# Keys and queries of a gated delta rule turned by VectorE instead of TensorE, gates as one ScalarE operation, and a new order of the mixer's work

## The chip, the cores and the metric

The kernel runs on one core of one Trainium2 chip. The metric is the device time of one execution in microseconds (us), the median of several runs. The engines are TensorE (PE; its weight loads are listed as PEld), VectorE (DVE), ScalarE (ACT), GpSimd (POOL) and SyncE (SP), which only issues transfers here.

## What is computed

One decoder layer of 512 tokens and width 1024: a SwiGLU feed-forward block, a hybrid mixer and a second feed-forward block, each behind an RMS norm. Of the reference, the part of the mixer that the change touches:

```python
q_h = jax.nn.silu(hq) * HG_DK ** -0.5                       # HGRN branch, 8 heads
o_h = rmsnorm(o_h, hgrn_out_norm) * jax.nn.silu(hg)
qkv = jax.nn.silu(causal_short_conv(concat(gq, gk, gv), conv_w))   # 4 taps, 32 heads of 128
q_g = l2norm(cq) * GDN_DK ** -0.5                           # 8 query and 8 key heads
k_g = l2norm(ck)
o_g = gated_delta_chunked(q_g, k_g, cv, sigmoid(gb), g)     # 16 value heads, chunks of 64
o_g = rmsnorm(o_g, gdn_out_norm) * jax.nn.silu(gz)
y = sigmoid(gate_h) * (o_h @ w_branch_hgrn) + sigmoid(gate_g) * (o_g @ w_branch_gdn)
```

Here l2norm(x) = x * rsqrt(sum(x*x) + EPS) over the 128 elements of a head.

## The kernel before

**Stages.** The first feed-forward block runs from 0 to about 355 us, the mixer to about 1240 us, the second block to the end. Activations lie with features on partitions and 512 tokens in the free dimension. Dense products are made in three passes (fp32 split into a high and a low part): high by high (L192), low by high (L193) and high by low (L194), each a 128x128 weight tile against 512 tokens (256 in the feed-forward blocks and the HGRN values). A weight tile of 128x512 is loaded by SP into one of RB = 3 `raw` places, then split: ACT casts the high part (`whi`, L1868), DVE subtracts to give the low part (`wlo`, L1870); WB = 6 such pairs exist. A cast waits until PE has done with the pair that it overwrites. A dense product goes to one of two PSUM banks (tag "mm", tile `pmm`), which ACT or DVE must read before the next but one may start.

**Order in the mixer.** The whole mixer is written out in an order that the class `Desk` makes while the program is built. Each piece of work is a generator ("thread") that asks for events ("on"), for places ("get": the six 128x512 tiles "ta", PSUM banks, buffers), or for an engine for a booked time ("use", with `A`, `V` and `T_` giving ACT, DVE and PE); "lag" lets time pass, as for a transfer. `Desk.run` always takes the engine and thread that can start first by these booked times, and instructions stand on each engine in that order. Dense products have the lowest rank on PE and come in the order of the string `DENSE` (F, Q, D, B are HGRN projections; k, q, v, z those of the delta rule; y merge gates), as far as `choose` finds their needs met. PE work marked `Patient` lets dense work go first for up to WAIT = 4 us.

**The delta rule (GDN).** Eight pairs u = 0..7, each one key/query head and two value heads. `conv` (L1168) copies a projection out of PSUM (`ci`, L1174), does the first tap on ACT (`cy`, L1181), three more on DVE (L1184), a Tanh on ACT (L1187) and finishes SiLU on DVE as (tanh+1)*y (L1193, L1196); a value head is then turned by DVE (`turn`, L1205) and bounced through DRAM (`bounce`: SP stores it and loads it back turned, with LAG["turn"] = 6.5 us booked for each). `norms` turns each key and query head on PE (four 128x128 transposes into `ptk`, L1245); ACT copies the keys (`kn`, L1248) and squares four blocks with a row sum (L1252). `g_e` makes the decays: Abs and one Exp for each head. Then come the 64x64 inverses by doubling (`pq`, copies L1398 to L1419), and the recurrence over chunks (`pks`, `pw`, `pog`). At the end of a pair, ACT scales the output (L1535, four instructions for a head); for pairs 0 to 6 DVE turns it and it is bounced, for the last pair PE turns it (`pto`, L1549), DVE gates it (`on`, L1552), and ACT (`uh`, L1561) and DVE (`ul`, L1563) split it into slices 14 and 15 of the input of the closing product with `wbg`. Slices that were stored earlier come back as `og` and are split at L1653 and L1655. `zgate` (L1605) and `gate` (L1623) make SiLU of the output gates, again by Tanh on ACT and a second operation on DVE.

Of the kernel before, what the change touches and what calls it, by code (L numbers as in the profile page):

```python
# [11 lines left out]
AF = mybir.ActivationFunctionType  # L12
ALU = mybir.AluOpType
# [3 lines left out]
P = 128  # L17
# [14 lines left out]
LEVELS = (1, 2, 4, 8, 16)  # L32

DENSE = (
# [3 lines left out]
)  # L38
MERGE = (None, None, "a", "a", "b", "b", None, None)
WB = 6  # L40
# [13 lines left out]
FRESH = 5  # L54
LAG = dict(raw=3.5, gb=6.5, nb=6, m=7, out=6.5, back=6, turn=6.5)
EASE = 2.5
LANES = {"a": 2, "b": 2, "d": 1, "e": 1}


# [7 lines left out]
class Desk:  # L67
# [3 lines left out]


    def __init__(self, **places):
        self.left, self.at, self.idle, self.now = dict(places), {}, {}, 0.0
        self.busy, self.asked, self.cur, self.dense = [], [], None, False

    def start(self, rank, gen):
# [660 lines left out]
def mixer(tc, mp, e):  # L738
# [11 lines left out]
    def v3(ap, a):  # L750
        return ap.rearrange("p (a b) -> p a b", a=a)
# [165 lines left out]
    def h_q(i, pt, new):  # L917
        tag = ("fs", "ut")[i % 2]
        if new:
            yield "get", "ta", 1  # L920
            yield *A(512), 1
            th = ta("th")
            act.activation(th, pt, AF.Tanh, scale=0.5)
            yield "get", tag, 1
            yield *V(560), 1
            qq = hq[i] = place(tag, "qq", (P, NT, 192), 4)
            dve.scalar_tensor_tensor(qq[:, :, :P], v3(th, NT), 1.0, v3(pt, NT), op0=ALU.add, op1=ALU.mult)
            D.put("mm")
            D.put("ta")
            D.fire(("Q", i))  # L930
            return
        yield "get", "ta", 2
# [4 lines left out]
        D.put("mm")  # L937
        yield A(512)
        th = ta("th")
        act.activation(th, qs, AF.Tanh, scale=0.5)  # L940
        yield "get", tag, 1
        yield V(512)
        qq = hq[i] = place(tag, "qq", (P, NT, 192), 4)
        dve.scalar_tensor_tensor(qq[:, :, :P], v3(th, NT), 1.0, v3(qs, NT), op0=ALU.add, op1=ALU.mult)
        D.put("ta", 2)
        D.fire(("Q", i))

    def h_f(i, pt, new):
# [33 lines left out]
    def h_head(i):  # L982
# [151 lines left out]
        dve.tensor_scalar(rho, ss, 4.0 / P, 4.0 * EPS * 4.0 * P, op0=ALU.mult, op1=ALU.add)  # L1134
# [34 lines left out]
    def conv(k, i, pt, out, n):  # L1169

        yield "get", "ta", 2
        yield *A(512), 1
        ci = ta("ci", (P, T + 32))[:, :T + 3]
        act.copy(ci[:, 3:], pt)  # L1174
        D.put("mm")
        yield V(4)
        dve.memset(ci[:, :3], 0.0)
# [3 lines left out]
        act.activation(y, ci[:, :T], AF.Copy, scale=wc[0])  # L1181
        for j in range(1, 4):
            yield V(550)
            dve.scalar_tensor_tensor(y, ci[:, j:j + T], wc[j], y, op0=ALU.mult, op1=ALU.add)  # L1184
        yield A(512)
        th = ci[:, :T]
        act.activation(th, y, AF.Tanh, scale=0.5)  # L1187
        a, b = (v3(th, n), v3(y, n)) if n else (th, y)
        if k[0] in "qk" and k[1] > 3:
            yield "on", ("K", k[1] - 4)  # L1190
        yield V(512)
        if n:
            dve.scalar_tensor_tensor(out, a, 1.0, b, op0=ALU.add, op1=ALU.mult)  # L1193
            D.put("ta", 2)
        else:
            dve.scalar_tensor_tensor(y, a, 1.0, b, op0=ALU.add, op1=ALU.mult)  # L1196
            yield V(512)
            turn(th, y)
            D.put("ta")
            yield from bounce(f"vn{i}", th, out, "ta")  # L1200
        D.fire(k)

    def turn(out, x):

        dve.transpose(out.rearrange("p (f c j) -> p f c j", f=4, c=NT), x.rearrange("p (c i f) -> p f c i", c=NT, f=4))  # L1205
# [12 lines left out]

    def g_e(u, st):

        yield "on", "decays", *([("at", 2 * u + 1)] if u < 2 else ["more"]), *([("R", u - 4)] if u > 3 else []), \
            *([("E", u - 1)] if u else [])
        for i in range(2):
            hd_ = 2 * u + i
            yield "get", "gb", 1
            yield "use", "ACT", .1
            gb = places["gb"]("gb", (P, NT, P))
            act.dma_start(gb, gtd[hd_:hd_ + 1].rearrange("o (c b) -> o c b", c=NT).to_broadcast([P, NT, P]))
            yield "lag", LAG["gb"]
            a = G["at"][u % 4 * 2 + i]  # L1230
            for c in range(NT):
                yield A(200)
                act.activation(a[:, c], gb[:, c], AF.Abs, bias=gam[:, c, hd_:hd_ + 1], scale=-1.0)
            D.put("gb")
            yield A(512)
            act.activation(a, a, AF.Exp, scale=-1.0)
        D.fire(("E", u))

    def norms(u, i, kq, kn, sm):
        yield "on", ("kq"[i], u)  # L1240
        yield "get", "e", 1
        yield T_(Patient(.5))
        pt = ps("ptk", "e")
        for c in range(NT):
            pe.transpose(pt[:, c * P:(c + 1) * P], kq[:, c, i], ident)  # L1245
        if i == 0:
            yield A(512)
            act.copy(kn, v3(pt, NT))  # L1248
        for c in range(NT):
            yield A(300)  # L1250
            pc = pt[:, c * P:(c + 1) * P]
            act.activation(pc, pc, AF.Square, accum_out=sm[:, 0, 4 * i + c:4 * i + c + 1])  # L1252
        D.put("e")
        D.fire(("norm", u, i))

    def g_n(u, st):
# [9 lines left out]
        hs = slice(2 * u, 2 * u + 2)  # L1266
        rk = sm[:, 1, 0:4]
        yield V(4)
        dve.tensor_scalar(rk, sm[:, 0, 0:4], 4.0 * EPS, None, op0=ALU.add)
# [10 lines left out]
        dve.tensor_scalar(c2, c2, 0.5, None, op0=ALU.mult)  # L1280
        D.fire(("C", u))
        yield "on", ("q", u)
        yield "on", ("qm", 0), ("n2", u % 2)
# [145 lines left out]
    def g_rec(u, st):  # L1429
# [34 lines left out]
        for c in range(NT):  # L1464
# [36 lines left out]
            if c < NT - 1:  # L1501
# [5 lines left out]
                else:  # L1507
                    for i in range(2):
# [12 lines left out]
        dve.tensor_scalar(sm[:, 7, 0:4], sm[:, 0, 4:8], 4.0 * P * EPS, 16.0 * P * EPS * EPS, op0=ALU.mult, op1=ALU.add)  # L1521
        dve.scalar_tensor_tensor(v3(rho, 2), v3(ss, 2), 4.0 / P, sm[:, 7:8, 0:4].to_broadcast([P, 2, 4]),
                                 op0=ALU.mult, op1=ALU.add)
        yield "lag", EASE
        yield "use", "POOL", 1.4
# [79 lines left out]
    def zgate(i, pt):  # L1605

        g = G["gz"][i // 2 % 3].rearrange("p c b -> p (c b)")[:, i % 2 * T:i % 2 * T + T]
        yield *A(512), 1
        act.activation(g, pt, AF.Tanh, scale=0.5)
        yield *V(560), 1  # L1610
        dve.scalar_tensor_tensor(g, g, 1.0, pt, op0=ALU.add, op1=ALU.mult)
        D.put("mm")
        D.fire(("z", i))

# [7 lines left out]

    def gate(key, g, t, o):  # L1623

        yield "get", "thg", 1
        yield A(300)
        th = places["thg"]("thg", (P, 256))
        act.activation(th, o, AF.Tanh, scale=0.5)
        yield V(256)
        dve.scalar_tensor_tensor(g[:, t], th, 1.0, o, op0=ALU.add, op1=ALU.mult)  # L1630
        D.put("thg")
        D.put("mm")
        if t == 3:
            D.fire(key)
# [464 lines left out]
```

## Time and profile before

| | us |
|---|---|
| median of 3 runs | 1596.22 (1595.67 to 1598.09) |
| the profiled execution's own time | 1595.04 |
| its span | 1593.3 |
| PE busy | 1580.1 (99%) |
| DVE busy | 1140.4 (72%) |
| ACT busy | 843.1 (53%) |
| POOL busy | 407.7 (26%) |

The span reaches from the first to the last profiled instruction; the run's own time is 1.7 us longer. A row of a group view gives line, engine, operation, output<-input, count, then busy time in us, mean ns of one, and the idle time of the engine ahead of it with what ended it. Matmuls overlap: in a steady stream one of 128x512 starts every 0.23 us, though its row says 0.39. In rows of single instructions, the bracket holds the idle time ahead and its releaser.

### The profile page before, as it was taken

The page shows a single profiled execution, that of the slowest core. Times are in us where ns is not written, and L with a number is a line of the kernel's source. Part 1 is how long each engine was busy: PE and PEld are TensorE (multiplying, and loading weights), DVE is VectorE, ACT ScalarE, POOL GpSimd, SP SyncE. Part 2 cuts the span into 40 slices and gives each one's busy share as a digit, 9 for nine tenths or more (in the row PEclk, how much of TensorE's full clock was granted, in tenths as well). Part 3 has the DMA queues.
Part 4 walks back from the last instruction along what each step waited for, and adds up shares of the span by engine and source line. Part 5 has one row for each costly group of instructions (what it writes and reads, how often), then busy time and mean ns, then how long its engine had stood idle before and what let it go on. Part 6 is the DMA issues. An engine that isn't in the chain of part 4 may idle for free.

```text
span 1593.3 us, 28865 instructions
## 1 busy us (share of the span) xinstructions
PE 1580.1 (99%) x10464; PEld 1368.1 (86%) x10464; DVE 1140.4 (72%) x2217; ACT 843.1 (53%) x1905; POOL 407.7 (26%) x715
## 2 busy tenths in 40 slices
PE   9999999999999999999999999999999999999997
PEld 8899998888888888888878888888788899999886
DVE  6988786448858769746788988875545799888323
ACT  5756674335334344645776666665324566667322
POOL 0211212000312222065635776610001121121000
PEclk9999999999999999999999999999999999999999
DMA  5777873333213213555345536566544587787431
GB/s 183 168 163 158 177 172 97 118 114 113 81 54 94 57 51 101 153 156 152 109 140 166 151 120 191 180 202 215 153 141 132 135 199 183 173 183 194 135 102 53
DMA packets 144751, 223.90 MB, mean 141 GB/s; under 512 B 22224, under 2 KB 44368, under 8 KB 144608
## 3 DMA queue, kind: packets, MB, share of 16 engines
q1 hardware_dynamic: 127472, 191.15, 38.8%
q0 software_dynamic: 14400, 26.22, 10.5%
q10 hardware_dynamic: 2736, 4.68, 1.0%
q8 instruction: 82, 1.34, 0.3%
q14 instruction: 61, 0.50, 0.1%
HBM read 197.06 MB, written 24.94 MB: 139 GB/s over the span
## 4 chain that ended last, share of the span: by engine, by line
PE 88%; DVE 4%; DMA 3%; issue 2%; ACT 1%; POOL 0%; SPq 0%; POOLq 0%; DVEq 0%; ACTq 0%
PE pmm L192 16%; PE pmm L193 15%; PE pmm L194 15%; PE px L194 6%; PE px L192 6%; PE px L193 6%; PE pnat L192 4%; PE pnat L194 4%; PE pnat L193 4%; DMA wlo<-w1b 1%; PE pgq L1291 1%; PE pog L1499 1%; PE pw L1483 1%; PE pl L1054 1%; DMA raw<-wt 1%
## 5 line engine op out<-in xcount | busy, mean ns | idle before, releaser
L192 PE MATMUL pmm<-uh,whi 128*128 128x512 f32 x834 | 343.6, 412 | 1.4 <-ACT ci L1174 1.4
L194 PE MATMUL pmm<-uh,wlo 128*128 128x512 f32 x834 | 326.3, 391 | 0.0
L193 PE MATMUL pmm<-ul,whi 128*128 128x512 f32 x834 | 325.6, 390 | 0.5 <-DVE ul L1655 0.3
L194 PE MATMUL px<-xs,wlo 128*128 128x256 f32 x1008 | 285.9, 284 | 0.7 <-DVE wlo L311 0.3
L193 PE MATMUL px<-xs,whi 128*128 128x256 f32 x1008 | 285.2, 283 | 0.0
L192 PE MATMUL px<-xs,whi 128*128 128x256 f32 x1008 | 285.2, 283 | 0.0
L1868 ACT CAST whi<-raw 128x512 fp32r<-128x512 f32 x226 | 140.0, 620 | 219.1 <-PE pmm L193 184.1
L1870 DVE TENSOR_TENSOR wlo<-raw,whi 128x512 fp32r<-128x512 f32 x226 | 162.2, 719 | 115.4 <-ACT whi L1868 110.7
L194 PEld LDWEIGHTS px<-xs,wlo 128*128 128x128 f32 x1008 | 193.4, 192 | 1.6 <-DVE wlo L311 0.8
L192 PEld LDWEIGHTS px<-xs,whi 128*128 128x128 f32 x1008 | 193.5, 192 | 0.1
L193 PEld LDWEIGHTS px<-xs,whi 128*128 128x128 f32 x1008 | 193.5, 192 | 0.1
L194 PEld LDWEIGHTS pmm<-uh,wlo 128*128 128x128 f32 x834 | 156.5, 188 | 34.5
L192 PEld LDWEIGHTS pmm<-uh,whi 128*128 128x128 f32 x834 | 157.0, 188 | 32.5 <-ACT ci L1174 2.0
L193 PEld LDWEIGHTS pmm<-ul,whi 128*128 128x128 f32 x834 | 157.2, 188 | 29.8 <-DVE ul L1655 0.6
L332 ACT CAST whi<-sw 128x512 fp32r<-128x512 f32 x144 | 87.5, 613 | 91.6 <-DVE sw L369 72.3
L332 ACT CAST whi<-rw 128x512 fp32r<-128x512 f32 x153 | 94.3, 617 | 76.2 <-PE pnat L194 42.9
L311 DVE TENSOR_TENSOR wlo<-sw,whi 128x512 fp32r<-128x512 f32 x144 | 98.2, 682 | 0.0
L332 ACT CAST whi<-raw 128x512 fp32r<-128x512 f32 x71 | 42.5, 601 | 91.9 <-PE pmm L193 41.1
L337 POOL DMA_DIRECT2D wlo<-w1b x53 | 45.9, 867 | 168.7 <-ACT wlo L336 107.8
L311 DVE TENSOR_TENSOR wlo<-raw,whi 128x512 fp32r<-128x512 f32 x67 | 51.1, 778 | 48.4 <-ACT whi L332 48.4
L1342 POOL TENSOR_TENSOR fm<-gfs,gln 128x60 f32<-128x60 f32 (+24 forms) x155 | 65.8, 425 | 63.5 <-DMA gln<-hmask 42.1
L337 POOL DMA_DIRECT2D wlo<-w1a x47 | 40.9, 870 | 159.6 <-ACT wlo L336 128.5
(489 smaller groups left out, 3324.1 us busy)
## 6 DMA issues: line engine op xcount, KB each, us to landing
raw<-wt SPq DMA_DIRECT2D x160, 256.0 KB
rw<-w1b SPq DMA_DIRECT2D x80, 256.0 KB
rw<-w1a SPq DMA_DIRECT2D x74, 256.0 KB
wlo<-w1b POOLq DMA_DIRECT2D x53, 256.0 KB, 5.3
wlo<-w1a POOLq DMA_DIRECT2D x47, 256.0 KB, 5.0
raw<-w2a SPq DMA_DIRECT2D x36, 256.0 KB
raw<-wn SPq DMA_DIRECT2D x32, 256.0 KB
raw<-wbg SPq DMA_DIRECT2D x32, 256.0 KB
```

The source lines that it names most:

```text
L192: pe.matmul(pt, ah, bh, start=first, stop=False)
L193: pe.matmul(pt, ah, bl, start=False, stop=False)
L194: pe.matmul(pt, al, bh, start=False, stop=last)
L311: dve.tensor_tensor(lo, x, hi.bitcast(F32), op=ALU.subtract)
L332: act.copy(hi, x)
L337: pool.dma_start(lo, units[i].fold, accum_op=ALU.add)
L1054: pe.matmul(pl_[s0:s0 + 32, c * 16:(c + 1) * 16], ke[:, c * P + s0:c * P + s0 + 32], qv[:, c, r, :, 1], start=True, stop=True)
L1291: pe.matmul(pq[:, (c % 2) * 256:(c % 2) * 256 + 256], kq[:, c, 0], kq[:, c].rearrange("p a b -> p (a b)"), start=True, stop=True)
L1342: pool.tensor_tensor(tv, bc(m[:, j + 1:, j], w), t[:, j:j + 1, :w].to_broadcast([P, n, w]), op=ALU.mult)
L1483: pe.matmul(pw[:, hd2[i]], ut[:, 4 * i + c], xs[i], start=True, stop=True)
L1868: act.copy(hi, raw)
L1870: dve.tensor_tensor(lo, raw, hi.bitcast(F32), op=ALU.subtract)
```

## The change

1. **Order string.** `DENSE` is rewritten: in the HGRN part F and Q are no longer strictly in turn, and in the GDN part keys come ahead of queries.
2. **Desk.** A place used to be counted. Now `left` keeps the time at which each one comes free (the time of the thread that gave it up), and a thread that takes it cannot start before.
3. **SiLU in one operation.** `h_q`, `conv`, `zgate` and `gate` use ACT's Silu and no second DVE operation. Constants that had made up for the factor 2 of (tanh+1)*y change with it.
4. **First tap.** It moves from ACT (Copy with a scale) to DVE (tensor_scalar).
5. **Keys and queries.** With TURNED = (0, 1), `norms` no longer uses PE and PSUM: DVE turns the head into a "ta" tile `kt`, SP stores it and loads it back, ACT copies the keys from there and squares from there. The "ta" place is held from the turn to the last square.
6. **Decays.** The two Exp of a pair stand behind one booking of 4 us on ACT.

```diff
     def put(self, tag, n=1):
-        self.left[tag] += n
+        self.left[tag] += [self.cur.t if self.cur else self.now] * n
+        self.left[tag].sort()
...
-                elif kind == "get" and self.left[what[0]] >= what[1]:
-                    self.left[what[0]] -= what[1]
-                    th.t = max(th.t, self.now)
+                elif kind == "get" and len(self.left[what[0]]) >= what[1]:
+                    th.t = max([th.t, self.now] + self.left[what[0]][:what[1]])
+                    del self.left[what[0]][:what[1]]
...
-        yield A(512)
+        yield V(512)
         y = ta("cy")
-        act.activation(y, ci[:, :T], AF.Copy, scale=wc[0])
+        dve.tensor_scalar(y, ci[:, :T], wc[0], None, op0=ALU.mult)
...
-        yield A(512)
-        th = ci[:, :T]
-        act.activation(th, y, AF.Tanh, scale=0.5)
...
-        yield V(512)
+        yield A(512)
         if n:
-            dve.scalar_tensor_tensor(out, a, 1.0, b, op0=ALU.add, op1=ALU.mult)
+            act.activation(out, v3(y, n), AF.Silu)
...
-            yield A(512)
+        yield "use", "ACT", 4.0
+        for i in range(2):
+            a = G["at"][u % 4 * 2 + i]
             act.activation(a, a, AF.Exp, scale=-1.0)
...
+        if i in TURNED:
+            yield "get", "ta", 1
+            yield V(900)
+            x = ta("kt")
+            turn(x, kq[:, :, i])
+            yield from bounce(f"{'kq'[i]}n{u}", x, x)
+            x4 = x.rearrange("p (r c j) -> p c r j", r=4, c=NT)
+            if i == 0:
+                yield A(512)
+                act.copy(kn.rearrange("p c (r j) -> p c r j", r=4), x4)
+                D.fire(("kc", u))
+            for c in range(NT):
+                yield A(300)
+                act.activation(x4[:, c], x4[:, c], AF.Square, accum_out=sm[:, 0, 4 * i + c:4 * i + c + 1])
+            D.put("ta")
+            D.fire(("norm", u, i))
+            return
...
     def gate(key, g, t, o):
-        yield "get", "thg", 1
         yield A(300)
-        th = places["thg"]("thg", (P, 256))
-        act.activation(th, o, AF.Tanh, scale=0.5)
-        yield V(256)
-        dve.scalar_tensor_tensor(g[:, t], th, 1.0, o, op0=ALU.add, op1=ALU.mult)
-        D.put("thg")
+        act.activation(g[:, t], o, AF.Silu)
```

In whole numbers, from the two orders: PE's matmuls go from 9074 to 9010 (the 64 transposes into `ptk`), with the dense ones 7552 in both; the places at which small matmuls stand between dense ones go from 192 to 198; ACT's table loads go from 5 to 27; DVE's turns from 94 to 110; transfers issued by SP from 781 to 813. A line of code gets another number: L192, L193, L194 become L194, L195, L196; L1174 becomes L1168, L1187 becomes L1183, L1245 and the `ptk` operations have no successor on PE, L1535 becomes L1545, L1549 becomes L1559, L1561 becomes L1571, L1868 becomes L1871. Where the changed order says `x_...` or `h`, it is a shared buffer under the name of its first user.

On PE, before the change, the closing product with `wbg` at the mixer's end. `pto` is the turned head; the three products behind the shown group, on `uh` and `ul`, are the thirteenth slice, then come the fourteenth and fifteenth, made from the two turned heads. The other group of transposes stands 15 matmuls ahead of this one:

```order
L194 MATMUL pmm<-uh,wlo 128x512
L1549 MATMUL pto<-sq,on 128x128 x4
L192 MATMUL pmm<-uh,whi 128x512
L193 MATMUL pmm<-ul,whi 128x512
L194 MATMUL pmm<-uh,wlo 128x512
L192 MATMUL pmm<-uh,whi 128x512
```

The same place on PE with the change: the thirteenth slice, a group of transposes, the fourteenth slice, a group of transposes, the fifteenth:

```order
L194 MATMUL pmm<-uh,whi 128x512
L195 MATMUL pmm<-ul,whi 128x512
L196 MATMUL pmm<-uh,wlo 128x512
L1559 MATMUL pto<-sq,on 128x128 x4
L194 MATMUL pmm<-uh,whi 128x512
L195 MATMUL pmm<-ul,whi 128x512
L196 MATMUL pmm<-uh,wlo 128x512
L1559 MATMUL pto<-sq,on 128x128 x4
L194 MATMUL pmm<-uh,whi 128x512
```

Each turned head is now used by the very next dense matmul; before, the first was used 18 dense matmuls after it was turned and the second six.

On ACT, before the change, early in the GDN part, where the keys of a pair are copied (`x_8168<-ptk`), the 64x64 inverse of the pair ahead is copied (`acc`, `h`), an output is scaled (`gat`), and a projection leaves PSUM (`ci<-pmm`):

```order
L1248 COPY x_8168<-ptk 128x512
L1252 ACTIVATE ptk,sm<-ptk 128x128
L1868 CAST whi<-raw 128x512
L1410 COPY acc<-pq_9012 128x256
L1252 ACTIVATE ptk,sm<-ptk 128x128 x3
L1181 ACTIVATE cy<-ci,cs 128x512
L1419 COPY h<-pq_9052 64x4x64
L1868 CAST whi<-raw 128x512
L1174 COPY ci<-pmm 128x512
```

The same place on ACT with the change:

```order
L1871 CAST whi<-raw 128x512
L1244 COPY x_8031<-kt 128x512
L1545 ACTIVATE gat<-gat,sm 128x128 x4
L1420 COPY acc<-pq_8872 128x256
L1248 ACTIVATE kt,sm<-kt 128x4x32
L1871 CAST whi<-raw 128x512
L1545 ACTIVATE gat<-gat,sm 128x128 x4
L1429 COPY h<-pq_8916 64x4x64 x2
L1183 ACTIVATE h<-cy 128x4x128
L1168 COPY ci<-pmm 128x512
```

Two outputs of four scalings each now stand among these rows, between a cast and the copy that frees a PSUM bank. The cast at the top overwrites a pair whose last reader on PE stands about 18 dense matmuls ahead of the matmul that needs this bank. The copy of the keys and the squares read `kt`, which a transfer has to bring, where they read PSUM before.

More of the change, by code (lines that the diff above doesn't have):

```diff
@@ L56 @@
 EASE = 2.5
+TURNED = (0, 1)
 LANES = {"a": 2, "b": 2, "d": 1, "e": 1}
@@ L73, in __init__ @@
     def __init__(self, **places):
-        self.left, self.at, self.idle, self.now = dict(places), {}, {}, 0.0
+        self.left, self.at, self.idle, self.now = {k: [0.0] * n for k, n in places.items()}, {}, {}, 0.0
         self.busy, self.asked, self.cur, self.dense = [], [], None, False
@@ L919, in h_q @@
         if new:
-            yield "get", "ta", 1
+            yield "get", tag, 1
             yield *A(512), 1
[L922 to L925, printed above, removed]
             qq = hq[i] = place(tag, "qq", (P, NT, 192), 4)
-            dve.scalar_tensor_tensor(qq[:, :, :P], v3(th, NT), 1.0, v3(pt, NT), op0=ALU.add, op1=ALU.mult)
+            act.activation(qq[:, :, :P], v3(pt, NT), AF.Silu)
             D.put("mm")
-            D.put("ta")
             D.fire(("Q", i))
             return
-        yield "get", "ta", 2
+        yield "get", "ta", 1
         yield "on", "rbc"
@@ L937, in h_q @@
         D.put("mm")
+        yield "get", tag, 1
         yield A(512)
-        th = ta("th")
-        act.activation(th, qs, AF.Tanh, scale=0.5)
-        yield "get", tag, 1
-        yield V(512)
         qq = hq[i] = place(tag, "qq", (P, NT, 192), 4)
-        dve.scalar_tensor_tensor(qq[:, :, :P], v3(th, NT), 1.0, v3(qs, NT), op0=ALU.add, op1=ALU.mult)
-        D.put("ta", 2)
+        act.activation(qq[:, :, :P], v3(qs, NT), AF.Silu)
+        D.put("ta")
         D.fire(("Q", i))
@@ L1184, in conv @@
             dve.scalar_tensor_tensor(y, ci[:, j:j + T], wc[j], y, op0=ALU.mult, op1=ALU.add)
[L1185 to L1188 removed]
         if k[0] in "qk" and k[1] > 3:
             yield "on", ("K", k[1] - 4)
[L1191 removed]
+        yield A(512)
         if n:
[L1193 removed]
+            act.activation(out, v3(y, n), AF.Silu)
             D.put("ta", 2)
         else:
[L1196 removed]
+            act.activation(y, y, AF.Silu)
             yield V(512)
+            th = ci[:, :T]
             turn(th, y)
@@ L1203, in turn @@
     def turn(out, x):
-        dve.transpose(out.rearrange("p (f c j) -> p f c j", f=4, c=NT), x.rearrange("p (c i f) -> p f c i", c=NT, f=4))
+        dve.transpose(out.rearrange("p (f c j) -> p f c j", f=4, c=NT), v3(x, NT).rearrange("p c (i f) -> p f c i", f=4) if len(x.shape) < 3 else
+                      x.rearrange("p c (i f) -> p f c i", f=4))
     def bounce(name, x, out, tag=None):
@@ L1608, in zgate @@
         yield *A(512), 1
-        act.activation(g, pt, AF.Tanh, scale=0.5)
-        yield *V(560), 1
-        dve.scalar_tensor_tensor(g, g, 1.0, pt, op0=ALU.add, op1=ALU.mult)
+        act.activation(g, pt, AF.Silu)
         D.put("mm")
```

11 lines of the change are left out of this document (6 added, 5 removed), and 6 rows, old and new, of the table DENSE.

## The prediction

> **What bounds the kernel now.** The page comes first: the row of busy times, and the chain of work that ended last, by engine.
>
> ```profile
> PE 1580.1 (99%) x10464; PEld 1368.1 (86%) x10464; DVE 1140.4 (72%) x2217; ACT 843.1 (53%) x1905; POOL 407.7 (26%) x715
> PE 88%; DVE 4%; DMA 3%; issue 2%; ACT 1%; POOL 0%; SPq 0%; POOLq 0%; DVEq 0%; ACTq 0%
> ```
>
> PE is busy 99% of the span and holds 88% of the chain. A change can therefore gain in two ways only: by PE instructions that go, and by PE waits that go. It loses by PE waits that come. The table of engine time by stretch shows where there is room on the others (length, PE, PEld, DVE, ACT, POOL; then clock, transfer share, GB/s):
>
> ```profile
> 360.00:660.00 300.00, 300.00 (x2578) 248.32 (x2578) 235.81 (x584) 127.46 (x310) 62.44 (x71) 1.00 0.27 81
> 660.00:1130.00 470.00, 466.99 (x2861) 384.37 (x2860) 355.25 (x747) 292.92 (x827) 228.89 (x512) 1.00 0.53 161
> ```
>
> PE is full in both stretches of the mixer; in the second it misses 3.0 us. DVE has 115 us free there and ACT 177. The clock is 1.00, so no time is to be had from it. PE's waits, in the view of who waited for whom:
>
> ```profile
> PE pmm L192 <- ACT ci L1174: 1.4, 1, 1.4
> PE pog L1497 <- ACT acc L1388: 0.5, 1, 0.5
> PE pmm L193 <- DVE ul L1655: 0.3, 1, 0.3
> PE pmm L193 <- DVE ul L1563: 0.2, 1, 0.2
> ```
>
> All waits of the mixer are of this size: one of 1.4 us, the rest under a microsecond. So there is little to gain by a better order, and every wait that a new order makes is a loss.
>
> **The change part by part.** *Transposes gone.* Each of 8 key and 8 query heads loses four transposes on PE.
>
> ```profile
> L1245 PE MATMUL ptk<-sq,h 128*128 128x128 f32 x48 | 7.3, 274 | 0.0
> ...
> 702.35 0.23 PE pmm L194
> 702.58 0.44 PE ptk L1245 x4
> 703.01 0.24 PE pmm L192
> ```
>
> The chain view shows what a group takes of PE's time, start to start: 0.44 us, less than four times the row's 274 ns, since they overlap. There are 48 + 16 of them, so 16 groups: 16 x 0.44 = **-7.0 us**. No other work could hide this, as PE does nothing else meanwhile. Six more places at which small work breaks the dense stream cost some 0.03 us each (the first dense matmul behind takes 0.24 instead of 0.23, and the small ones overlap less): +0.2 us.
>
> *The wait that the Desk's new bookkeeping removes.* PE's largest wait:
>
> ```profile
> 824.83 1.08 DVE L1205 STREAM_TRANSPOSE ci<-cy 128x512 f32<-128x512 f32 x1
> 825.94 0.59 ACT L1174 COPY ci<-pmm 128x512 f32<-128x512 f32 x1 [1.28 <-DVE ci L1205]
> 826.58 0.50 PE L192 MATMUL pmm<-uh,whi 128*128 128x512 f32 x1 [1.41 <-ACT ci L1174]
> ```
>
> The copy out of PSUM had to wait until a "ta" place was truly empty, which the order had counted as free already. With times kept for places, the copy is put where the place is free. The dense matmul ahead starts at 824.78 and would be followed 0.23 later, at 825.01; it is 826.58, so **-1.6 us**. At worst the same wait returns elsewhere (0).
>
> *The mixer's tail.* Before, one turned head had 18 dense matmuls of cover and the other six. Now both have none. The rows of the second head show the chain that a head has to go through:
>
> ```profile
> 1119.70 0.39 PE L192 MATMUL pmm<-uh,whi 128*128 128x512 f32 x1
> 1120.39 0.60 PE L1549 MATMUL pto<-sq,on 128*128 128x128 f32 x4
> 1121.62 0.75 DVE L1552 SCALAR_TENSOR_TENSOR on<-pto,cs,ggz 128x512 f32<-128x512 f32 x1
> 1122.46 0.62 ACT L1561 CAST uh<-on 128x512 fp32r<-128x512 f32 x1 [1.54 <-DVE on L1552]
> 1123.11 0.69 DVE L1563 TENSOR_TENSOR ul<-on,uh 128x512 fp32r<-128x512 f32 x1 [0.74 <-ACT uh L1561]
> 1123.86 0.50 PE L193 MATMUL pmm<-ul,whi 128*128 128x512 f32 x1 [0.23 <-DVE ul L1563]
> 1124.43 0.39 PE L192 MATMUL pmm<-uh,whi 128*128 128x512 f32 x1
> ```
>
> Transposes 0.60, 0.05 to DVE, 0.75, 0.09 to ACT, 0.62, 0.05 to PE: 2.16 us to the high part, and 0.73 more (`ul` 0.69 and 0.04 around it) to the low part, 2.89 in all. Without a wait that matmul starts 0.44 + 0.23 = 0.67 behind the first transpose. A head thus costs 2.2 us and two cost 4.4. From 1119.70 to 1124.43 there are 4.73 us, for 12 dense matmuls of 0.23 and one group of 0.44, 3.2 us: before lost about 1.5 here already. The difference is **+2.9 us**. The closing products of other output blocks can't step in: PE works in the order written. The low end is 2.4, if ACT and DVE start as soon as released and overlap, the high end 4.4, if a weight split of 0.69 stands in front on DVE for each.
>
> *A burst on ACT.* In the order of the change, early in the GDN part, ten rows of ACT stand from a weight cast to the copy that frees a PSUM bank. What they take, by their counterparts before:
>
> ```profile
> L1868 ACT CAST whi<-raw 128x512 fp32r<-128x512 f32 x226 | 140.0, 620 | 219.1 <-PE pmm L193 184.1
> ...
> L1248 ACT COPY gkn<-ptk x6: 562/587/592, 556.4 to 908.7; 128x512 f32<-128x512 f32 x6
> ...
> 1108.83 1.28 ACT L1535 ACTIVATE on<-gqm,sm 128x128 f32<-128x128 f32 x4
> ...
> L1410 ACT COPY acc<-pq x8: 369/373/390, 734.3 to 1061.4; 128x256 f32<-128x256 f32 x8
> ...
> L1252 ACT ACTIVATE ptk<-ptk 128x128 f32<-128x128 f32 x64 | 16.8, 263 | 2.7 <-PE ptk L1245 1.4
> ...
> L1419 ACT COPY h<-pq x6: 367/368/371, 777.9 to 1065.3; 64x256 f32<-64x256 f32 x6
> ...
> L1187 ACT ACTIVATE ci<-cy 128x512 f32<-128x512 f32 x32 | 20.1, 628 | 12.8 <-DVE cy L1184 11.2 <-DVE ci L1177 1.5
> ...
> L1174 ACT COPY ci<-pmm 128x512 f32<-128x512 f32 x32 | 18.6, 582 | 3.9 <-DVE h L1193 1.4 <-DVE ci L1205 1.3 <-DVE x L1193 1.0
> ```
>
> Two casts 1.24, the keys 0.59, two times four scalings 2.56, `acc` 0.37, one square 0.26, two copies `h` 0.74, the Silu at Tanh's 0.63, the copy 0.58: 7.0 us. As the row of casts shows, they wait for PE (184.1 of 219.1 us of idle time), so the first cast can't start early: it waits for a matmul that stands in the order about 18 dense matmuls (18 x 0.23 = 4.2 us) ahead of the one that needs the bank. PE then waits 7.0 - 4.2, with the hand-over about **+2.9 us**. The low end is 0 (the squares and scalings overlap, or the cast was released earlier); the high end twice that, as one more place has two outputs close together.
>
> *Silu and the first tap.* These move work between ACT and DVE.
>
> ```profile
> L1181 ACT ACTIVATE cy<-ci,cs 128x512 f32<-128x512 f32 x32 | 22.9, 720 | 8.1 <-DVE ci L1177 5.3 <-issue 1.8 <-ACT ci L1174 0.6
> L966 DVE TENSOR_SCALAR f<-fs,cf 128x512 f32<-128x512 f32 x8 | 4.3, 542 | 0.1
> L1205 DVE STREAM_TRANSPOSE ci<-cy 128x512 f32<-128x512 f32 x16 | 17.6, 1097 | 0.2
> ```
>
> ACT loses 32 taps (22.9 us); DVE gains 32 at the 0.54 of its nearest row (17.3 us) and 16 turns of 1.1 us (17.6), and loses an operation for every Silu, 32 in `conv` alone. Neither engine's stretch gets fuller by anything that its 115 and 177 free microseconds don't hold. Nothing is taken for it: what hides it is PE's own work of 227 ns a matmul. Without that cover each 0.1 us later at a PSUM copy would be 0.1 us later on PE.
>
> *Table loads.* Silu and Exp stand in turn on ACT, which adds 22 loads.
>
> ```profile
> 1247.53 0.63 ACT L336 ACTIVATE wlo<-whi 128x512 fp32r<-128x512 f32 x1
> 1248.17 1.28 ACT L484 ACT_TABLE_LOAD   x1
> 1249.47 0.63 ACT L484 ACTIVATE fa<-fa 128x512 f32<-128x512 f32 x1
> ```
>
> A load takes 1.28 us, and the instruction behind starts 0.02 later; with the 0.1 by which two activations would have overlapped, 1.4 each and 31 us in all. By PE's waits, none of the five loads before held PE, so 0 is taken; 31 is the other end. [...]
>
> *Bounces of keys and queries.* 32 more transfers of 256 KB on SP's queue, and ACT's copy and squares wait for the reload, with weight casts and PSUM copies behind them in ACT's queue. The nearest rows are the values, bounced in the same way:
>
> ```profile
> L1350 DVE TENSOR_TENSOR gvb<-gvb,sm 128x512 f32<-128x512 f32 x12 | 8.4, 700 | 6.6 <-DMA gvb<-vn 6.6
> ```
>
> Their 12 reloads held DVE for 6.6 us, 0.55 each; 16 would hold ACT for 8.8. No wait of PE above names such a reload, so 0 is taken and 8.8 kept.
>
> **Sum** against the profiled execution: -7.0 + 0.2 - 1.6 + 2.9 + 2.9 = -2.6, so 1595.04 - 2.6 = 1592.4. The median of the runs shown is 1.2 above the profiled execution: **1593.6 us**.
>
> **The rivals.** *A: the new waits don't show.* The tail's head is turned early enough by slack on PE, and ACT's burst fits. For it: before, the waits are all small. Against: nothing stands between a head's turn and its use. -7.0 + 0.2 - 1.6 = -8.4, median 1587.8.
>
> *B: the reloads are late, and ACT stands.* This ends slower. Place: the key copy and squares on ACT; price 0.55 us a bounce; it decides when a PSUM copy or cast that PE needs stands behind within the cover of some 4 us. For it: the values' 6.6 us, and 32 more transfers in a stretch where the queues are busy 53%. Against: ACT has 177 us free. -2.6 + 8.8 = +6.2, median 1602.4.
>
> *C: loads hold PE.* If each of 22 loads stands in front of what PE waits for, -2.6 + 31 = +28, median 1625. Against: the pairs of Exp stand together, and ACT idles 38% of the stretch. [...]
>
> *D: the change takes the transposes but gets nothing for it:* the keys come by two transfers later than by PE, so a pair starts later, and PE lacks small work to fill with and waits at the end for what it had spared (7.0 back): +4.4, median 1600.6. Against: PE's dense stream goes on meanwhile.
>
> **How the numbers follow.** Forecast 0.45, with its own range 1590.5 to 1597; A 0.27, B 0.16, D 0.10, C 0.02. The range runs from 1586, A with a microsecond or two more, to 1602.5, B. What a measurement can tell from no change is 0.2%, 3.2 us, so faster is under 1593.0. The forecast lies near that line: 0.18 faster, 0.27 the same. A is faster; B is slower but for 0.02, C slower, D slower by 0.07 and the same by 0.03. Together 0.45, 0.32 and 0.23.
>
> **What would show it.** Right: no `ptk` rows on PE; PE's waits name `uh` and `ul` of the last two heads with about 4 us in all near 1115 us, and a `ci` copy with about 3 us near 770 us; the wait at 826 is gone; 27 loads of 1.28 us. Wrong: those waits are missing (A); ACT's key copy and squares show idle time ended by a transfer, and PE waits behind them (B); PE's waits name an activation that follows a load (C); the last pair's recurrence ends later against the dense stream (D).

## The result and the profile after

The changed kernel takes **1602.5 us** (median of 7 runs, 1599.8 to 1605.3) against 1595.7 before; the ratio is 1.0039, 95% interval 1.0029 to 1.0050. It is slower by 0.4%, where 1593.6 us was forecast and a faster kernel held the highest chance. The profiled execution took 1602.48 us, 7.4 more than that of before.

The page of the changed kernel, the row of engines and the clock in 40 slices (tenths):

```profile
PE 1580.1 (99%) x10400; PEld 1365.4 (85%) x10400; DVE 1128.5 (70%) x2185; ACT 845.1 (53%) x1895; POOL 400.7 (25%) x715
...
PEclk9999999999999999999899999999999999999999
```

PE has 64 instructions fewer (10400 for 10464, the same difference as between the 9074 and 9010 given above) and is busy for exactly as long as before. Something made the others longer, and the one 8 in the clock's row points to it. The stretches of the mixer (length, PE, PEld, DVE, ACT, POOL; clock, transfer share, GB/s):

```profile
660.00:1130.00 470.00, 458.90 (x2774) 375.42 (x2773) 346.45 (x727) 287.89 (x807) 221.45 (x512) 0.99 0.55 173
1130.00:1260.00 130.00, 130.00 (x576) 107.69 (x576) 62.97 (x96) 45.70 (x74) 10.68 (x9) 0.98 0.47 145
```

PE's waits, in total, times and longest:

```profile
PE pmm L194 <- ACT ci L1168: 3.8, 4, 1.9
PE pmm L194 <- ACT uh L1571: 3.1, 2, 1.5
PE pq L1405 <- ACT acc L1398: 2.6, 1, 2.6
PE pw L1493 <- ACT h L1429: 1.3, 1, 1.3
```

In the stretch from 660 to 1130 us PE is idle for 11.1 us, where it was 3.0: +8.1. And the clock, 1.00 in both stretches before, is 0.99 and 0.98. Three places hold all of the lost clock and 9.7 of the 11.1 us. The first two, in stretches of 2 us (length, PE busy and instructions, clock, transfer share, GB/s):

```profile
754.00:756.00 2.00, 1.90 (x9) 1.00 0.95 222
756.00:758.00 2.00, 0.00 (x0) 1.00 0.91 299
758.00:760.00 2.00, 0.69 (x32) 0.93 0.39 105
760.00:762.00 2.00, 0.98 (x2) 0.50 0.27 95
762.00:764.00 2.00, 2.00 (x6) 0.50 0.49 188
764.00:766.00 2.00, 2.00 (x6) 0.50 0.19 74
766.00:768.00 2.00, 2.00 (x22) 0.87 0.00 0
```

PE stands from 755.9 to 761.0, with 32 small matmuls in between, and then runs at **half clock** until about 766.5: six matmuls in 2 us instead of nine. The second place, at 770 to 773 us, is the burst that the prediction had priced. The third is the tail; PE's rows there:

```profile
1123.21 0.60 PE L1559 MATMUL pto<-sq,on 128*128 128x128 f32 x4
1125.36 0.50 PE L194 MATMUL pmm<-uh,whi 128*128 128x512 f32 x1 [1.55 <-ACT uh L1571]
1126.08 0.50 PE L195 MATMUL pmm<-ul,whi 128*128 128x512 f32 x1 [0.23 <-DVE ul L1573]
1126.42 0.39 PE L196 MATMUL pmm<-uh,wlo 128*128 128x512 f32 x1
1126.65 0.60 PE L1559 MATMUL pto<-sq,on 128*128 128x128 f32 x4
1128.80 0.80 PE L194 MATMUL pmm<-uh,whi 128*128 128x512 f32 x1 [1.55 <-ACT uh L1571]
...
1130.54 0.63 PE L194 MATMUL pmm<-uh,whi 128*128 128x512 f32 x1
1130.97 0.63 PE L195 MATMUL pmm<-ul,whi 128*128 128x512 f32 x1
```

Each head is turned and waited for, as predicted. But the matmuls behind start every 0.43 us instead of 0.23, and they do so until 1135.2. The engine's row says "busy" through all of it, as it does from 762 to 764 us: 2.00 us, with six matmuls. Counted by their starts, 11 matmuls behind the first stall, 5 behind the second and 11 behind the third ran with 0.2 us more each, and with the slower ones at both ends the half clock costs 2.7 + 1.6 + 2.7 = 7.0 us.

So the 7.4 us come together: -7.0 for the transposes, +8.1 of idle time, +7.0 of half clock make +8.1. The 0.7 too much is not traced further (the feed-forward stretches differ by tenths in both directions).

Why PE stood at 757 is in ACT's and SP's rows:

```profile
751.71 0.19 ACT L1469 ACTIVATION_READ_ACCUMULATOR sqj<-gat 128x1 f32 x1
757.16 0.62 ACT L1871 CAST whi<-raw 128x512 fp32r<-128x512 f32 x1 [5.26 <-DMA raw<-wt]
757.68 0.73 ACT L1398 COPY acc<-pq 32x256 f32<-32x256 f32 x2
758.43 1.28 ACT L1183 ACT_TABLE_LOAD   x1
759.73 0.63 ACT L1183 ACTIVATE x<-cy 128x512 f32<-128x512 f32 x1
760.38 0.59 ACT L1168 COPY ci<-pmm 128x512 f32<-128x512 f32 x1
```

```profile
745.92 0.34 SPq L1203 DMA_DIRECT2D kn<-kt  x1
746.91 0.32 SPq L1203 DMA_DIRECT2D vn<-ci  x1
747.36 2.96 SPq L1340 DMA_DIRECT2D gfs<-nb  x4
750.38 0.43 SPq L1346 DMA_DIRECT2D gln<-hmask  x1
750.92 1.50 SPq L1829 DMA_DIRECT2D raw<-wt  x3
```

ACT waits 5.3 us for a weight, and behind that cast stand the copy of the inverse, a table load, a Silu and the copy that frees a PSUM bank, all of which PE needs. The weight was late on SP: ahead of it in the queue stand two stores of turned heads, each of which waits for its turn on DVE (SP stands 3.3 us for the first), four loads `gfs` (3 us of issue) and one more. It was issued at 750.9, and ACT's cast of it began 6.2 us later; from 752 to 758 the transfer engines were 91 to 96% busy.

### The profile page after: what moved, and what is told of

It is laid out like the page before. It is cut to its first block, busy times and chain, and to the rows that moved or that the text cites. A ratio compares the mean times of both kernels' runs of the same rounds, so it can differ in the third digit from the quotient of the medians.

```text
span 1600.7 us, 28744 instructions
## 1 busy us (share of the span) xinstructions
PE 1580.1 (99%) x10400; PEld 1365.4 (85%) x10400; DVE 1128.5 (70%) x2185; ACT 845.1 (53%) x1895; POOL 400.7 (25%) x715
## 5 line engine op out<-in xcount | busy, mean ns | idle before, releaser
L194 PE MATMUL pmm<-uh,whi 128*128 128x512 f32 x834 | 348.0, 417 | 7.0 <-ACT ci L1168 3.8
L195 PE MATMUL pmm<-ul,whi 128*128 128x512 f32 x834 | 328.5, 394 | 0.2 <-DVE ul L1573 0.2
L196 PE MATMUL pmm<-uh,wlo 128*128 128x512 f32 x834 | 328.7, 394 | 0.0
L196 PE MATMUL px<-xs,wlo 128*128 128x256 f32 x1008 | 285.7, 283 | 0.5 <-DMA wlo<-w1a 0.2
L195 PE MATMUL px<-xs,whi 128*128 128x256 f32 x1008 | 285.3, 283 | 0.0
L194 PE MATMUL px<-xs,whi 128*128 128x256 f32 x1008 | 285.2, 283 | 0.0
L1871 ACT CAST whi<-raw 128x512 fp32r<-128x512 f32 x226 | 139.0, 619 | 143.3 <-PE pmm L195 104.2
L196 PEld LDWEIGHTS px<-xs,wlo 128*128 128x128 f32 x1008 | 193.5, 192 | 1.2 <-DMA wlo<-w1a 0.4
L194 PEld LDWEIGHTS px<-xs,whi 128*128 128x128 f32 x1008 | 193.5, 192 | 0.1
L195 PEld LDWEIGHTS px<-xs,whi 128*128 128x128 f32 x1008 | 193.5, 192 | 0.1
L194 PEld LDWEIGHTS pmm<-uh,whi 128*128 128x128 f32 x834 | 158.7, 190 | 39.5 <-ACT ci L1168 5.2
L196 PEld LDWEIGHTS pmm<-uh,wlo 128*128 128x128 f32 x834 | 158.1, 190 | 35.1 <-DVE wlo L615 0.2
L195 PEld LDWEIGHTS pmm<-ul,whi 128*128 128x128 f32 x834 | 158.9, 191 | 29.7 <-DVE ul L1573 1.0
L1352 POOL TENSOR_TENSOR fm<-gfs,gln 128x60 f32<-128x60 f32 (+24 forms) x155 | 60.9, 393 | 51.6 <-DMA raw<-wt 18.1
```

The costliest lines, as they stand in the source:

```text
L194: pe.matmul(pt, ah, bh, start=first, stop=False)
L195: pe.matmul(pt, ah, bl, start=False, stop=False)
L196: pe.matmul(pt, al, bh, start=False, stop=last)
L1352: pool.tensor_tensor(tv, bc(m[:, j + 1:, j], w), t[:, j:j + 1, :w].to_broadcast([P, n, w]), op=ALU.mult)
L1871: act.copy(hi, raw)
```

## The experiments

The theory from these rows: **two stalls, one near 757 us and one in the tail, and the half clock behind each, are the loss**. The rivals: table loads on ACT; the turns and transfers themselves; the order as such.

**e1, the tail alone.** The last two heads are turned together, and slices 14 and 15 of the first two output blocks go behind slices 12 and 13 of both.

```diff
-            yield T_(Patient(.5))
+            yield T_(.5)
...
+            D.start((4, u, i), head(i, og))
+            continue
...
+                for k in (14, 15):
+                    for x in (0, 1):
+                        yield "on", ("so", k)
+                        yield T_(.69)
+                        piece(x, k)
```

> The changed kernel, with only the mixer's tail altered: the last two heads are turned one right behind the other, and in the closing product's first two output blocks slices 12 and 13 of both blocks stand ahead of slices 14 and 15, so that each turned head has some 6 to 12 matmuls of cover. The result is the same sum in another order. Theory (stalls and the clock behind them): PE's two waits at 1123 to 1129 us (1.7 us each, with 0.5 for each low part, 4.4 in all) shrink to under 1 us, and with them the stretch of half clock from 1128 to 1135 goes, 15 matmuls at 0.43 instead of 0.23: 3.1 more. About 1602.5 - 3.6 - 3.1 = 1595.8. Rival (the half clock isn't caused by the waits): only the waits go, about 1598.9, and the clock is still half there.

Measured: 1595.7 us, 0.9998 of before (0.9988 to 1.0008). No wait of the tail's splits over 0.4 us is left and no matmul there starts 0.43 us behind the one ahead; the stall at 757 stays (3.1 and 1.9 us in this trace). The tail was worth 6.8 us: 4.4 of waits, of which some 0.4 stay, and about 3 of half clock (the clock from 1130 to 1260 us is 1.00 for 0.98). This is the theory's number, not the rival's.

**e2, no turns, no transfers.** In the changed order, ACT reads the unturned heads.

```diff
-            turn(x, kq[:, :, i])
-            yield from bounce(f"{'kq'[i]}n{u}", x, x)
+            yield S
+            yield "lag", LAG["turn"]
+            yield S
+            yield "lag", LAG["turn"]
...
```

> The changed kernel with the same order of everything else, but DVE's 16 turns of keys and queries and their 32 transfers are left out; ACT copies and squares the unturned heads. The output isn't the layer's: keys and queries enter untransposed. Theory (the burst near 757 us begins with DVE and SP: weights come late because DVE's turns push back the low parts that free their buffers, and the transfers share the queues): ACT's wait of 5.3 us for a weight at 752 to 757 shrinks by 2 to 3 us, PE's stall there from 4.8 us to 2 or less, and the half clock behind it goes: 1602.5 - 2.7 - 3 = about 1597. Rival (table loads make the burst): no change beyond 1 us, 1601 to 1604.

Measured: 1600.1 us, 1.0025 (1.0012 to 1.0037), between the two numbers. PE's first wait near 757 falls from 2.6 to 1.7 us, the second stays at 1.9, and so does the half clock (0.99 from 660 to 1130 us, as in the changed kernel). The work that the turns add costs 2.4 us by the medians, hardly clear of noise, as this interval overlaps that of the changed kernel; most of the stall stands without it.

**e3, no table loads.** The same order with Tanh in the place of Silu.

```diff
-            act.activation(out, v3(y, n), AF.Silu)
+            act.activation(out, v3(y, n), AF.Tanh)
...
```

> The changed kernel in the same order, with Tanh in the place of every Silu, so that ACT needs almost no table loads more than before. The output isn't the layer's: all gates and the convolutions' results are tanh(x). Theory (stalls and clock; a load costs only where PE waits behind ACT at that moment): one load of 1.3 us stands inside the stall near 757 us, so 1.3 us, and at most 3 more if the half clock goes with it: 1598 to 1601; the tail's waits of 4.4 us and their half clock stay. Rival (the loads are the loss: 22 x 1.4 us of ACT, partly in front of PE): 10 us or more, below 1592.

Measured: 1599.1 us, 1.0018 (1.0008 to 1.0028), in the theory's range. PE's waits for `ci` fall from 3.8 to 2.4 us, by one load's time; the other waits stay. The trace has 3 loads where the changed kernel has 27: 24 loads of 1.28 us cost 3.4 us by the medians, not 31. PE's waits show 1.4 of this. The half clock of the tail is also shorter in this trace (0.99 for 0.98 from 1130 to 1260 us) behind the same waits, so not all of the 3.4 need be the loads'.

**e4, PE turns the heads again.** TURNED = (), all else as changed; the order comes out anew.

> The changed kernel with keys and queries turned by PE as before (TURNED empty); order string, place times, Silu, first tap and grouped Exp stay. The order of the mixer is made anew by that. Theory: the 16 groups of transposes come back (+7.0 us), the stall near 757 us with its half clock goes (-8), and the tail's first head has 18 matmuls of cover again, the second none: half of 4.4 and perhaps the half clock go (-2 to -5): 1595 to 1600. Rival (the turned keys are not what hurts; order string or place times are): the stalls stay and the time is 1606 or more.

Measured: 1591.5 us, 0.9973 (0.9962 to 0.9984), less than expected. With the 64 transposes back PE is idle for only 1.1 us from 660 to 1130, and the clock is 1.00 throughout:

```profile
660.00:1130.00 470.00, 468.90 (x2874) 1.00 0.52 161
```

One wait of PE in the mixer is over a quarter of a microsecond, 0.7 us. So the rest of the change, in this order, gains some 4 us on before, and turning by DVE, with the order that comes of it, makes that a loss of 7.

**e5, only queries by DVE.** TURNED = (1,).

> The changed kernel with only the queries turned by DVE (TURNED = (1,)); the keys are turned by PE as before. Theory (the loss is made by stalls of one order, above all where the keys' later arrival moves the inverse, the recurrence and the tail; queries are needed later and cost nothing but space): 8 groups of transposes fewer than with PE turning both (1591.5), -3.5, and no stall over 2 us: about 1588 to 1590. Rival (any turn through memory fills DVE and the queues and brings stalls): PE waits near 757 us as in the changed kernel, with half clock, 1597 or more.

Measured: 1595.5 us, 0.9995 (0.9985 to 1.0004). The theory's number fails: a new stall stands elsewhere.

```profile
659.24 0.58 ACT L1627 COPY yh<-pmm 128x512 f32<-128x512 f32 x1 [3.30 <-DMA vn<-ci]
```

The copy out of PSUM waits for a "ta" tile that a turned value head's store still holds (issued at 652.35, 6.9 us ahead of the copy). PE waits 4.1 us for that copy, and 13 matmuls run at half clock behind the wait (the mean clock of this execution is 0.996, of the kernel before's 0.999).

**e6, single Exp.** Each Exp stands behind its own head's Abs, without the booking of 4 us.

```diff
-        yield "use", "ACT", 4.0
-        for i in range(2):
-            a = G["at"][u % 4 * 2 + i]
+            yield A(512)
             act.activation(a, a, AF.Exp, scale=-1.0)
```

> The changed kernel with each Exp behind its own head's Abs again, in place of two behind one booking of 4 us. The order is made anew. Theory A (the booking of 4 us pushes weight casts back, and the burst near 757 us begins there): that stall goes with its half clock, the tail's stays, 1602.5 - 5 - 3 = 1594 to 1596. Theory B (the burst comes from where the turned keys put their work): a stall of 3 us or more remains between 740 and 790 us, 1600 to 1606.

Measured: 1618.8 us, 1.0148 (1.0133 to 1.0164), worse than either theory. The new order has single waits of 2.4 to 3.1 us at 654, 830, 883 and 1137 us, and four stretches of half clock (the mean clock of the execution is 0.989); behind the first, ACT loads tables twice within 2 us (656.39 and 658.33, for an Exp and the Silu behind it). With this order string the order made without the booking is worse. As the whole order is another, the run says nothing on the stall at 757.

**e7 and e8, a wait of known length.** The kernel before, with operations that do nothing in the chain of the last head.

```diff
+            if i:
+                for _ in range(4):
+                    dve.tensor_scalar(og, og, 1.0, None, op0=ALU.mult)
```

The theory, that a wait of some 2 us already costs the clock, stands here against the rival that only the longer one does.

> The kernel before, with four DVE operations of 0.5 us (times one, in place) in the chain of the very last turned head, between its gating and its split: PE's wait for that head's high part, 0.4 us before, becomes about 2.4, behind a smaller wait of about 1 us some 2 us earlier. No other order changes. Theory (the clock falls when PE stands for a good part of some 3.4 us, though not for all of it): +2.0 of waiting and, in most executions, 1.5 to 3 more for a stretch of half clock behind it: 1599.7 to 1601, and matmuls at 0.43 us behind the wait. [...]

> The kernel before, with eight such operations: PE's wait becomes about 4.4 us. Theory and rival both have the clock fall to a half: +4 of waiting and 1.5 to 3 more, 1601.5 to 1603. If the clock doesn't fall here, waits are not what lowers it, and the time is 1600.

Measured: with four, 1597.9 us, 1.0016 (1.0007 to 1.0025), the runs spread from 1594.8 to 1600.4; with eight, 1601.5 us, 1.0040 (1.0025 to 1.0055). In the profiled execution of the first (1599.5 us), PE's idle time ahead of the late head is 1.8 us and of the second 3.6. The clock behind each, of the first:

```profile
1126.00:1128.00 2.00, 1.68 (x4) 0.61 0.00 0
1128.00:1130.00 2.00, 2.00 (x7) 0.54 0.00 0
1130.00:1132.00 2.00, 2.00 (x10) 1.00 0.45 131
```

and of the second:

```profile
1126.00:1128.00 2.00, 0.00 (x0) 0.70 0.00 0
1128.00:1130.00 2.00, 1.79 (x4) 0.50 0.00 0
1130.00:1132.00 2.00, 2.00 (x6) 0.50 0.00 0
1132.00:1134.00 2.00, 2.00 (x7) 0.59 0.47 131
```

Nothing but a wait was added, and the half clock follows it: the waits cause it. One of 1.8 us was enough in this execution. The median of e7 is the rival's number (the added wait alone, about 1598), so it seems that its runs don't all pay: their mean clocks are 0.997 to 0.999. The trace is of one that did, at 0.998.

**e9 and e10, parts on the kernel before.** The place times alone, and with them the turning by DVE; old order string, Tanh, tap on ACT.

> The kernel before with the Desk's place times alone (an order made anew; nothing else of the change). Theory: PE's wait of 1.4 us at 826 us goes, and the order is else as good: 1593 to 1595. Rival (any new order costs as much as it gains): 1596 to 1600, with waits of PE over 1.5 us elsewhere.

> The kernel before with place times and with keys and queries turned by DVE; Tanh, the tap on ACT, single Exp and the old order string stay. Theory (turning through memory makes the keys, and so the last pair's recurrence, late; the tail's two heads stand right ahead of their use in this order too): 7 us of transposes gone, but the tail waits 4.4 us with a half clock of 2 to 3 behind, and one more stall of 2 us or more in the middle: 1595 to 1602. Rival (the changed kernel's loss comes from its order string or Silu): the tail costs 4.4 us and nothing else is lost, 1592 or less.

Measured: 1608.9 us, 1.0077 (1.0063 to 1.0091), and 1629.9 us, 1.0208 (1.0193 to 1.0224). Both expectations fail by far. The wait at 826 is gone, but with place times the old order string gives waits of 1.1 to 2.0 us in a row near 810 and 840 us, and with the turning on top waits of 2.2 to 2.9 us at 839, 894, 901 and 948, and of 4.2 us in the tail. A likely reading is that place times make the booked order truer, but a string made for the old bookings no longer fits; the new string with the old bookings was not run.

**e11, three in one.** e1, e2 and e3 together.

> The first three experiments in one: the changed kernel's order with the tail's heads ahead, no turns and transfers of keys and queries, and Tanh in place of Silu. The output isn't the layer's. It is the changed order without the work that it added. Theory (added work and order share the stall near 757 us): the single effects add up, 1602.5 - 6.8 - 2.4 - 3.4 = 1590, with at most one wait of over 1.5 us left near 757 us; under 1588 if the half clock goes there too. Rival (the order alone makes that stall): 1592 or more.

Measured: 1592.5 us, 0.9979 (0.9967 to 0.9991), by 0.5 us on the rival's side of the line. The order without the added work still waits near 757:

```profile
756.33 0.62 ACT L1893 CAST whi<-raw 128x512 fp32r<-128x512 f32 x1 [4.48 <-DMA raw<-wt]
```

and PE behind it:

```profile
PE pq L1408 <- ACT acc L1401: 1.8, 1, 1.8
```

ACT's wait for the weight falls from 5.3 to 4.5 us only, and SP still stands 3.3 us for the value head that it has to store. Of the 4.4 us that PE stood near 757 in the changed kernel, 2.4 stay (1.8, and 0.6 for `ci`): these come of the order without the added work. The table load made 1.3 (e3) and the turns 0.8 (e2).

**e12, PE's turns with e1's tail.**

> The changed kernel with PE turning keys and queries (1591.5) and the tail's two heads turned ahead of slices 12 and 13. In the former PE loses about 1 us in the tail (waits 0.2 and 0.2, 0.5 behind for the low part): 1590.5 to 1591.5. It would beat both kernels.

Measured: 1591.3 us, 0.9969 (0.9958 to 0.9981): as e4, within the runs' spread.

**e13 and e14, SP relieved at the one place.** The four `gfs` loads of the third pair are issued by GpSimd; e14 has e1's tail too.

```diff
-            sp.dma_start(m[32 * b:32 * b + 32].rearrange("p i j -> p (i j)"),
+            (pool if u in (2,) else sp).dma_start(m[32 * b:32 * b + 32].rearrange("p i j -> p (i j)"),
```

> The changed kernel, in which the four loads gfs of the third pair alone are issued by GpSimd (idle there) in place of SP; nothing else moves. Theory (the stall near 757 us is made on SP: the weights that ACT waits for stand behind two stores of turned heads that wait for DVE, and behind these four loads of 0.6 us of issue each): the weights are issued at about 747.4 instead of 750.9, ACT's wait of 5.3 us falls to 2 or less, PE's stall of 2.6 + 1.9 us to about 1, and the half clock from 760 to 766 us goes: 1602.5 - 3.5 - 3 = 1596. Rival (the weights' buffers or the transfers' own time set it): under 1 us of gain, ACT's wait still over 4 us.

> The same with the tail of the first experiment too: both stalls out of the changed order, keys and queries still turned by DVE. Theory: the two effects add, 1595.8 - 6.5 = 1589.3, less than PE turning them (1591.3): then DVE's turns do gain once the order around them has no stall. Rival: 1593 or more.

Measured: 1595.7 us, 0.9998 (0.9989 to 1.0008), and **1590.3 us, 0.9965 (0.9951 to 0.9978)**, the fastest here. ACT, GpSimd, SP and PE of e13:

```profile
752.76 0.62 ACT L1871 CAST whi<-raw 128x512 fp32r<-128x512 f32 x1 [0.28 <-PE pmm L195]
...
742.97 2.37 POOL L1340 DMA_DIRECT2D gfs<-nb  x4 [5.51 <-DMA nb<-gn]
...
750.02 1.69 SPq L1829 DMA_DIRECT2D raw<-wt  x3
...
757.61 0.50 PE L194 MATMUL pmm<-uh,whi 128*128 128x512 f32 x1 [0.50 <-ACT ci L1168]
```

The cast no longer waits for a weight, and PE's stall of 2.6 + 1.9 us is 0.5. The times fit the theory, its working only in part: the weights are issued 0.9 us sooner, not 3.5 (they now wait for their buffers). The rest is that the `gfs` loads started 4.4 us sooner and were out of the way: a weight that had taken 6.2 us from issue to cast takes at most 2.7. The transfer engines show it. Here are length, PE, clock, transfer share and GB/s from 744 to 750 us, first of the changed kernel and then of e13:

```profile
744.00:750.00 6.00, 6.00 (x28) 1.00 0.31 115
744.00:750.00 6.00, 6.00 (x28) 1.00 0.80 235
```

While SP stood for the turned heads, the transfer engines were 31% busy, and then everything came at once; in e13 the `gfs` loads use that time. The run moves them to another queue and to an earlier time together, and doesn't tell these apart. That the total is the theory's is partly luck: in this trace the half clock behind the burst is gone too and the tail's is shorter (1.00 for 0.98 from 1130 to 1260 us), with the same waits there, while the second feed-forward block takes about 1.4 us longer.

By their ratios e14 (0.9965) and e12 (0.9969) can't be told apart, so the gain over turning by PE that was expected of e14 isn't shown.

## Why the prediction was wrong

- *Transposes gone, -7.0.* Right as far as the rows go: no `ptk` row on PE. The time was not measured apart.
- *The wait at 826 goes, -1.6.* Right, though a smaller one of 1.1 us comes at 877 us.
- *Tail, +2.9.* Right: 2.2 us a head were predicted, 1.7 for the high part and 0.5 for the low were measured. The chain of single rows, added up, was good to a tenth.
- *Burst on ACT, +2.9.* Right in place; its size was 2.0 (1.3 ahead of `pw`, 0.6 ahead of the next product).
- *Table loads, 0.* By e3 they cost 3.4 us in this order, above the value taken and far below the other end of 31; one load stood in front of PE inside the stall at 757.
- *Bounces, 0.* The cost was bounded by late reloads, at the values' 0.55 us. In the trace ACT waits 0.2 us for a reload, once. What the bounces do stands elsewhere: their stores wait in SP's queue for DVE, with weights behind (e2: 2.4 us with the turns, hardly clear of noise).

Two steps failed. The first is a **missing term**: the sum looked for waits that the change makes in ACT's and PE's order, and took none for SP's queue. The stall at 757 (4.4 us of PE's time) came from there. SP stood behind a store that waited for its turn on DVE, so four loads were issued 4.4 us later than in e13, and the weights came while the transfer engines were 91 to 96% busy: the weight was issued only 0.9 us late but took 6.2 us to its cast, where 2.7 are enough. SP's order around the third pair's `gfs` was to be had beforehand. The second is the sentence "The clock is 1.00, so no time is to be had from it": no time was to be gained, but there was time to be **lost**. In its trace, the kernel before had no wait over 1.6 us and kept its clock at 1.00. The three stalls that the change made cost 1.6 to 1.8 times their waits, with 7.0 us of half clock in all. For the predicted stalls alone (1.6 + 2.7) that term would have turned -2.6 into about +2. The stall at 757 and its half clock (4.4 + 2.7) make it about +9; the burst was 0.9 smaller than forecast, and the last 0.5 down to the measured +7.4 is not traced.

Rival B named the right time, 1602.4, by a wrong cause: ACT stood for a weight, and for a reload only 0.2 us. Rival D had a part of the truth: in the tail the last recurrence product starts at 1108.7, 14.5 us ahead of the first `pto`; before it was 20, at 1096.5. Rival C is out by e3.

## What to carry to other kernels

Where TensorE is full, count each new wait with its aftermath: the three stalls here cost 1.6 to 1.8 times their waits, as the clock stood at 0.50 behind each, so that one of 2 us would cost an estimated 3.2 to 3.6. Read the order of the issuing queue as closely as that of the engines: a store that waited 3.3 us for its data held the loads behind it here, and the transfer engines went from 31% busy (744 to 750 us) to 91 to 96% (752 to 758). And before dropping work from the full engine, look for the stalls that the new order brings; with both removed, the change went from 7 us of loss to over 5 of gain (e14). Of the 7.0 us that the transposes take on PE, e14 keeps at most about 1.0 against e12, within the noise; 3.4 went to idle time from 660 to 1130 us (4.2 against 0.8), and the rest isn't traced.

## What the runs showed of the hardware

Three times in the mixer of the changed kernel's trace PE's clock fell from 1.00 to 0.50: at 759.7 us, at 773.4 and at 1128.4. The waits there were 2.6 and 1.9 us (757), 1.3 and 0.6 with four small matmuls between (770), and two of 1.55, 3.4 us apart (the tail). PE was not wholly idle ahead of any of the three: it was busy for 0.69, 1.70 and 1.67 of the last 3.4 us. In the profiled executions of e7 and e8 the clock fell at a wait of 1.8 us and at one of 3.6. It stayed at 1.00 at one of 1.1 us (877 us; PE busy for 2.32 of the 3.40 us from 875.5), and of 1.4 us at 825 in the kernel before (1.99 of the 3.40 us from 823.2). From the clock of each 2 us (a row at 0.61 has 0.39 / 0.5 x 2 = 1.6 us of half clock), the half clock lasted 3.4 us in e7 and 6.8 in e8, and by the same view 6.8, 3.4 and 6.8 at the three places of the changed kernel.

The same waits didn't cost the clock in every run. The burst of 1.3 and 0.6 us, in the changed kernel (length, PE, clock, transfer share, GB/s), the 3.4 us ahead of the fall and the half clock itself:

```profile
769.95:773.37 3.42, 1.70 (x21) 1.00 0.35 102
773.37:776.78 3.41, 3.18 (x8) 0.50 0.65 237
```

In e13 the clock stayed at 1.00 over the same two waits:

```profile
762.59:766.00 3.41, 2.24 (x24) 1.00 0.52 156
766.00:769.41 3.41, 2.63 (x12) 1.00 0.66 196
```

In e11 and e14, with the same wait of 1.3 us, the clock from 660 to 1130 us reads 1.00, in the changed kernel 0.99.

The changed kernel's own runs differ in their clock too: three took 1599.8 to 1600.4 us at a mean clock of 0.996, and four 1602.5 to 1605.3 at 0.993. Only one of these runs has a trace, so what decides whether a wait of 1 to 2 us costs the clock wasn't shown.
